# A two-layer encoder on one core: a settled pair's first copy of u goes behind the second product's cast and sum, and two products of the down projections change places

## The chip, the cores and the metric

The kernel runs on one core of a Trainium2 chip. Five engines take part: TensorE (PE; its weight loads are shown as PEld), VectorE (DVE), ScalarE (ACT), GpSimd (POOL) and SyncE (SP, which here only issues DMAs). The metric is the device time of one execution in microseconds (us), as the median of several runs.

## What is computed

The reference is a trunk of two layers over two groups of tokens, 512 and 256, with 1024 features, all in float32. Four of its six phases are feed-forward networks (FFN) of one form:

```python
def swiglu(h, wg, wu, wd):
    return (jax.nn.silu(h @ wg) * (h @ wu)) @ wd

x = x + 0.5 * swiglu(rmsnorm(x, f1_n), f1_g, f1_u, f1_d)
x = x + mixer(rmsnorm(x, mix_n), ...)
x = x + 0.5 * swiglu(rmsnorm(x, f2_n), f2_g, f2_u, f2_d)
```

The inner width is 2816. The mixer of layer 0 joins a gated unit and windowed attention, that of layer 1 is a neighbourhood attention; the change doesn't touch them. A last `rmsnorm` ends the trunk.

## The kernel before

**Precision.** A float32 product is made of three passes. An operand is split into a high part (`whi` for weights, a cast on ScalarE, line 122) and a low part, the operand less its high part (`wlo`, a subtraction on VectorE, line 123). The passes are high by high, high by low, low by high (`mm3`). So a weight block must be cast before the first pass, and its low part made before the third matmul. `whi` and `wlo` have five buffers each. Operands of the activations are split in the same manner by `split` (lines 208 and 209).

**Fewer products.** A pair of 128-wide blocks of the inner width, times two halves of 384 tokens, forms a 2x2 block product. It is done with seven products instead of eight (Winograd's form of Strassen's method). The seven are named after their activation operand: b11, b21, t1, t2, t3, n4, b22. The weight operand of some is a sum, made on VectorE by `sums` (line 739): s1 = a21 + a22, s2 = s1 - a11, s3 = a11 - a21, s4 = a12 - s2 (in the buffer of s2). Products t2, t3, t1, b22 take s2, s3, s1, s4; n4 takes a22. The profile leaves numbers out of names, so that s1, s2 and s4 are all "s"; s3's buffer is "s" too.

**An FFN** has 11 pairs of columns (`pair(p)`), each for `gate` and `up`. The first four pairs are early: their b11 and b21 products run first, and the rest is done in `settle`, in the order t2, t3, n4, t1, b22, gate before up in each. While gate's product runs, `parts` makes the weight operand of the next one. After a t2 or t3 product, `keep` copies the bank into an SBUF tile u (line 573, ScalarE) and takes one step of `operands(p - 1)`. Those steps make the activation operands that the previous pair gives to the down projection: each is a `put` (a cast and a subtraction, lines 208 and 209) or a `sub` (line 497). In the profile these operands are db (b11, b21, b22), dt (t1, t2, t3) and dn (n4). The s1 sums of an early pair come ready from DMAs issued by GpSimd, which add as they write, so that its s2 is one subtraction.

**Down projections.** After pairs 2, 4, 6, 8 the `down` of two finished pairs runs (pairs 0 and 1 behind pair 2, and so on); behind pair 9 stands a `down` of pair 8 alone. It loads two rows of weights for each pair (`raw`, four buffers, issued by SP): row 0 holds a11 and a21, row 1 holds a12 and a22. It makes the seven products for four output blocks each: t1 on banks Z, b11 and b21 on banks X, t2 and t3 on banks Y, b22 on banks W, n4 on banks Y. Y begins as a copy of X, W as a copy of Y after t2. The results are added to the tiles x (line 795, VectorE). X and W lie in PSUM pool `mm`, Y and Z in `aux`; each pool has four banks. The next stage begins with products in `mm`. In the first FFN, SP also issues small loads for bias tables between the others (lines 1634 and 1639).

**Order.** Only TensorE's instructions keep the order in which the code traces them (`manual_schedule` for PE). Those of the other engines are put in order when the program is built, by the framework's scheduler, which goes by readiness and by the order of tracing. `issue_after(ins)` makes the instructions traced in its block follow `ins` where they are on the engine of `ins`; it sets an order in the queue and no wait between engines.

Of the kernel before, what the change touches and what calls it, by code (L numbers as in the profile page):

```python
# [14 lines left out]
ALU = mybir.AluOpType  # L15
# [40 lines left out]
class Trunk:  # L56
# [55 lines left out]
    def wsplit(self, src, eng=None, keep=False):  # L112

        nc = self.nc
        self.pi += 1
        if keep:
            hi, lo = (self.fw.tile([P, 512], F32R, tag="s", name=f"k{n}{self.pi}", bufs=8) for n in ("hi", "lo"))
        else:
            hi = self.wp.tile([P, 512], F32R, tag="whi", name=f"whi{self.pi}")
            lo = self.wp.tile([P, 512], F32R, tag="wlo", name=f"wlo{self.pi}")  # L120
        hi, lo = (t.rearrange("p (a b) -> p a b", a=src.shape[1]) for t in (hi, lo))
        nc.scalar.copy(hi, src)  # L122
        (eng or nc.gpsimd).tensor_tensor(out=lo, in0=src, in1=hi.bitcast(F32), op=ALU.subtract)  # L123
        return hi, lo

# [243 lines left out]
    def etile(self, name):  # L369
        return self.fw.tile([P, H], F32, tag="e", name=name, bufs=NE)  # L370
# [107 lines left out]
    def ffn(self, pre):  # L478
        nc = self.nc
# [36 lines left out]
        def operands_2(h, sub, put):  # L516
            h11, h12, h21, h22 = h[0, 0], h[0, 1], h[1, 0], h[1, 1]
            yield put("t2", h11)
            yield sub(h12, h22, h12)
            yield put("t3", h12)  # L520
            yield put("b22", h22)
            yield sub(h21, h21, h11)
            yield put("n4", h21)

        entries, entered, addeds = {}, {}, {}

        def pair(p):
# [13 lines left out]
            s, bank, e = {}, {}, {}  # L541
# [5 lines left out]
            def parts(n, b):  # L547
                name = {"t2": "s2", "t3": "s3", "t1": "s1", "b22": "s4"}.get(b)
                with self.tc.high_priority() if b == "t2" and p in urgent else nullcontext():
                    return self.wsplit(sums(n, name) if name else a[n, 2, 2], nc.vector)  # L550
# [19 lines left out]
            def keep(out, key, n):  # L570

                e[n, out] = etile(out)
                nc.scalar.copy(e[n, out], bank[key, n])  # L573
                next(steps, None)

            def add(key, n, other):
                t = e[n, other]
                nc.vector.tensor_tensor(out=t, in0=bank[key, n], in1=t, op=ALU.add)  # L578
                next(steps, None)

            def hidden(i, half, g, u):

                self.run_until(lambda: half in scales)
                h[i, half] = t = g if half else etile("sg")
                v = u if half else etile("v")
                r = rt[:, HALVES[half][0] : HALVES[half][1]]
                nc.vector.tensor_tensor(out=t, in0=g, in1=r, op=ALU.mult)
                nc.scalar.activation(t, t, AF.Silu)
                self.freed = nc.vector.tensor_tensor(out=v, in0=u, in1=r, op=ALU.mult).ins
                nc.vector.scalar_tensor_tensor(out=t, in0=t, scalar=0.5, in1=v, op0=ALU.mult, op1=ALU.mult)  # L590

            def begin(n, p1):

                bank["Y", n] = self.psum()[:, :H]
                nc.scalar.copy(bank["Y", n], p1)
# [56 lines left out]
            def settle(st):  # L652

                todo = [(n, b) for b in ("t2", "t3", "n4", "t1", "b22") for n in names]
                key = {"t1": "Z", "b22": "Z"}
                for i, (n, b) in enumerate(todo):
                    now, st = st, None
                    if i + 1 < len(todo):
                        st = parts(*todo[i + 1])
                    elif p + 1 < EARLY and (p % 2 or not p):  # L660
                        entered[p + 1] = entries[p + 1]()
                    if b == "t2":
                        begin(n, e[n, "p1"])
                    product(n, None, b, key.get(b, "Y"), b == "t1", now)
                    if b in ("t2", "t3"):
                        keep(b.replace("t", "u"), "Y", n)
                    elif b == "n4":
                        next(steps, None)
                    else:
                        add("Z", n, "u3" if b == "t1" else "u2")  # L670
                    if n == "up":
                        if b == "n4":
                            hidden(1, 0, bank["Y", "gate"], bank["Y", "up"])
                        elif b == "t1":
                            hidden(1, 1, e["gate", "u3"], e["up", "u3"])
                        elif b == "b22":
                            hidden(0, 1, e["gate", "u2"], e["up", "u2"])
# [59 lines left out]
    def sums(self, a11, a12, a21, a22, s, n, name):  # L737

        f = lambda o, x, y, op: self.nc.vector.tensor_tensor(out=o, in0=x, in1=y, op=op)  # L739
        if name == "s1":  # L740
            return s[n, "s1"]
        if name == "s2" and (n, "s1") in s:
            t = s[n, "s2"] = self.fw.tile([P, 4, P], F32, tag="s", name="s2", bufs=8)
            f(t, s[n, "s1"], a11, ALU.subtract)
            return t
        if name == "s4":
            t = s[n, "s2"]
            f(t, a12, t, ALU.subtract)
            return t
        if name == "s2":  # L750
            t = s[n, "s1"] = self.fw.tile([P, 4, P], F32, tag="s", name="s1", bufs=8)
            f(t, a21, a22, ALU.add)
        t = s[n, name] = self.fw.tile([P, 4, P], F32, tag="s", name=name, bufs=8)
        if name == "s3":
            f(t, a11, a21, ALU.subtract)
        else:
            f(t, s[n, "s1"], a11, ALU.subtract)
        return t
# [4 lines left out]
    def down(self, pre, pairs, d, acc, then=None):  # L763

        nc = self.nc
        a, s, bank = {}, {}, {}
        for p in pairs:
            rows = [self.raw(f"{pre}_w_down", 2 * p + k, 1, 0, D)[:, 0, :] for k in (0, 1)]  # L770
            a[p] = [t[:, i * 512 : (i + 1) * 512].rearrange("p (a b) -> p a b", a=4) for i in (0, 1) for t in rows]
        sums = lambda name: {p: self.sums(*a[p], s, p, name) for p in pairs}

        def product(w, b, key, start, out, to=None):

            st = {p: self.wsplit(w[p], nc.vector) for p in pairs}
            for j in range(4):
                new = lambda k: (self.psum(self.aux, "aux") if k in "YZ" else self.psum())[:, :H]
                if start:
                    bank[key, j] = new(key)  # L780
                ps = bank[key, j]
                for p in pairs:
                    self.mm3(
                        ps, (st[p][0][:, j, :], st[p][1][:, j, :]), d[p][b],
                        start and p == pairs[0], p == pairs[-1], not start,
                    )
                if to:
                    bank[to, j] = new(to)
                    nc.scalar.copy(bank[to, j], ps)
                if out:  # L790
                    o = acc[j] if out is acc else self.x[4 * out[0] + j][:, HALVES[out[1]][0] : HALVES[out[1]][1]]
                    if out is acc and pairs[0] == 0:
                        nc.scalar.copy(o, ps)
                    else:
                        nc.vector.tensor_tensor(out=o, in0=ps, in1=o, op=ALU.add)  # L795

        def more(n):
            for _ in range(n if len(pairs) > 1 else 0):
                next(self.later, None)

        w = {n: {p: a[p][i] for p in pairs} for i, n in enumerate(("a11", "a12", "a21", "a22"))}
        s2 = sums("s2")
        if then:
            then()
        product(sums("s1"), "t1", "Z", True, acc)
        product(w["a11"], "b11", "X", True, None, "Y")
        more(3)
        product(w["a12"], "b21", "X", False, (0, 0))
        more(1)
        product(s2, "t2", "Y", False, None, "W")  # L810
        more(3)
        product(sums("s3"), "t3", "Y", False, (1, 1))
        product(sums("s4"), "b22", "W", False, (0, 1))
        product(w["a22"], "n4", "Y", False, (1, 0))

    def last_operands(self, d, k0, h, acc=None):

# [1008 lines left out]
```

## Time and profile before

| | us |
|---|---|
| median of 3 runs | 2592.65 |
| lowest and highest | 2589.17, 2595.09 |
| the profiled execution, its own time | 2590.38 |
| span of the profiled execution | 2588.6 |
| mean granted TensorE clock in it | 0.996 |

A line of the timeline gives the start, the duration, the engine, the line of the kernel, the operation, the tile written and those read, and how many were merged; in brackets stands the idle time of the engine before it, and what ended it. In a window row each engine's busy time stands with the number of its instructions. The first FFN fills the span from its start to about 515 us, the second 780 to 1250, the third 1250 to 1740, the fourth 2100 to the end.

### The profile page before, as it was taken

To read this page: it belongs to the slowest core of one execution; us is meant where nothing else is said; L and a number is where in the kernel's file an instruction comes from. 1 tells how busy PE (TensorE), PEld (TensorE's weight loads), DVE (VectorE), ACT (ScalarE), POOL (GpSimd) and SP (SyncE) were. 2 spreads that over 40 slices of the span, in tenths; PEclk is the share of its full clock that TensorE was granted. 3 is DMA by queue.
4 is the path that set the end of the run, shared out by engine and by line. 5 is a ranking of instruction groups with operands and counts; after the bars stand their busy time and mean duration, and the time that the engine had idled before them with its cause. 6 is when DMAs were issued, how large, how long until landed. Compare 5 with 4: busy or idle time off the path is not lost.

```text
span 2588.6 us, 41317 instructions
## 1 busy us (share of the span) xinstructions
PE 2552.2 (99%) x15114; PEld 2487.2 (96%) x15114; DVE 2232.6 (86%) x4662; ACT 1366.6 (53%) x2869; POOL 155.5 (6%) x252
## 2 busy tenths in 40 slices
PE   8999999999999999999999999999999999999998
PEld 8999999988899999999999999998998999999997
DVE  7988898978879989889998889886776699888897
ACT  7544454646656545445654445454455575444543
POOL 1000000000021000000100000001222220000000
PEclk9999999999999999999999999999999999999999
DMA  7523222331144322222542222242221343222222
GB/s 246 170 81 106 72 74 74 124 100 46 58 125 132 114 66 74 74 66 98 136 109 82 66 77 71 66 145 64 64 64 41 106 134 119 82 74 74 71 66 76
DMA packets 93372, 238.68 MB, mean 92 GB/s; under 512 B 21488, under 2 KB 34288, under 8 KB 93168
## 3 DMA queue, kind: packets, MB, share of 16 engines
q1 hardware_dynamic: 85712, 218.96, 26.3%
q0 software_dynamic: 7168, 16.78, 3.1%
q8 instruction: 119, 1.95, 0.3%
q14 instruction: 85, 0.70, 0.1%
q10 hardware_dynamic: 288, 0.29, 0.0%
HBM read 226.56 MB, written 15.07 MB: 93 GB/s over the span
## 4 chain that ended last, share of the span: by engine, by line
PE 89%; DVE 6%; ACT 2%; DMA 1%; issue 1%; SPq 0%; DVEq 0%; ACTq 0%
PE ps_mm L152 54%; PE ps_aux L152 34%; PE ps_aux L156 1%; DVE wlo L123 1%; ACT p L1109 1%; DVE p L1103 1%; DMA raw<-in_w 1%; DVE tl L209 0%; DMA x<-in_x 0%; DVE tmp L415 0%; DVE p L1119 0%; ACT whi L122 0%; DVE s L739 0%; DMA first<-in_w 0%; DVE o L1254 0%
## 5 line engine op out<-in xcount | busy, mean ns | idle before, releaser
L122 ACT CAST whi<-s 128x512 fp32r<-128x512 f32 x496 | 304.6, 620 | 407.3 <-DVE s L739 177.6
L122 ACT CAST whi<-raw 128x512 fp32r<-128x512 f32 x504 | 306.1, 619 | 222.9 <-PE ps_mm L152 91.3
L123 DVE TENSOR_TENSOR wlo<-s,whi 128x512 fp32r<-128x512 f32 x496 | 336.8, 684 | 61.0 <-ACT whi L122 53.4
L123 DVE TENSOR_TENSOR wlo<-raw,whi 128x512 fp32r<-128x512 f32 x471 | 321.7, 691 | 18.2 <-ACT whi L122 14.5
L152 PE MATMUL ps_mm<-db,whi 128*128 128x384 f32 x864 | 219.2, 334 | 0.0
L152 PE MATMUL ps_aux<-dt,whi 128*128 128x384 f32 x864 | 219.2, 334 | 0.0
L152 PEld LDWEIGHTS ps_aux<-dt,whi 128*128 128x128 f32 x864 | 156.0, 188 | 0.0
L152 PEld LDWEIGHTS ps_mm<-db,whi 128*128 128x128 f32 x864 | 156.0, 188 | 0.0
L152 PE MATMUL ps_mm<-xh,whi 128*128 128x512 f32 (+1 forms) x416 | 146.2, 352 | 0.0
L152 PE MATMUL ps_aux<-dt,wlo 128*128 128x384 f32 x432 | 144.4, 334 | 1.4 <-DVE wlo L123 1.4
L152 PE MATMUL ps_mm<-db,wlo 128*128 128x384 f32 x432 | 144.3, 334 | 0.0
L152 PE MATMUL ps_mm<-xh,wlo 128*128 128x512 f32 (+1 forms) x416 | 141.3, 340 | 0.0
L152 PE MATMUL ps_mm<-xl,whi 128*128 128x512 f32 (+1 forms) x416 | 141.2, 339 | 0.0
L739 DVE TENSOR_TENSOR s<-raw,raw 128x512 f32<-128x512 f32 x124 | 84.0, 685 | 25.7 <-DMA raw<-in_w 25.5
L578 DVE TENSOR_TENSOR u<-ps_aux,u 128x384 f32<-128x384 f32 x176 | 96.9, 550 | 4.9 <-PE ps_aux L152 4.8
L152 PE MATMUL ps_aux<-dh,whi 128*128 128x384 f32 x384 | 97.5, 334 | 0.0
L795 DVE TENSOR_TENSOR x<-ps_aux,x 128x384 f32<-128x384 f32 x160 | 85.3, 551 | 14.1 <-PE ps_aux L152 13.8
L1109 ACT ACTIVATE p<-p,st 128x256 f32<-128x256 f32 (+3 forms) x144 | 68.9, 480 | 49.3 <-DVE st L1107 49.2
L573 ACT COPY u<-ps_mm 128x384 f32<-128x384 f32 x176 | 83.5, 475 | 16.5 <-PE ps_mm L152 15.9
L795 DVE TENSOR_TENSOR x<-ps_mm,x 128x384 f32<-128x384 f32 x160 | 86.1, 550 | 7.1 <-PE ps_mm L152 6.8
L107 POOL DMA_DIRECT2D s<-in_w x64 | 47.1, 781 | 702.2 <-PE ps_aux L152 387.6
L152 PEld LDWEIGHTS ps_mm<-xh,whi 128*128 128x128 f32 x416 | 79.8, 192 | 9.3 <-issue 0.9
(516 smaller groups left out, 8134.1 us busy)
## 6 DMA issues: line engine op xcount, KB each, us to landing
raw<-in_w SPq DMA_DIRECT2D x346, 512.0 KB, 3.7
s<-in_w POOLq DMA_DIRECT2D x64, 256.0 KB, 5.0
xdm<-x SPq DMA_DIRECT2D x16, 384.0 KB, 2.4
x<-in_x SPq DMA_DIRECT2D x16, 192.0 KB, 6.3
tok<-in_xt SPq DMA_DIRECT2D x12, 256.0 KB, 6.5
xold<-xdm SPq DMA_DIRECT2D x8, 384.0 KB, 3.1
x<-xdm SPq DMA_DIRECT2D x8, 384.0 KB, 4.7
out_y<-y SPq DMA_DIRECT2D x8, 384.0 KB, 2.4
```

What stands on the lines that cost most here:

```text
L107: (eng or self.nc.sync).dma_start(raw, src, **kw)
L122: nc.scalar.copy(hi, src)
L123: (eng or nc.gpsimd).tensor_tensor(out=lo, in0=src, in1=hi.bitcast(F32), op=ALU.subtract)
L152: self.nc.tensor.matmul(out, lhsT=lhsT, rhs=rhs, start=start, stop=stop, **kw)
L156: self.nc.tensor.transpose(out, src, self.ident)
L573: nc.scalar.copy(e[n, out], bank[key, n])
L578: nc.vector.tensor_tensor(out=t, in0=bank[key, n], in1=t, op=ALU.add)
L739: f = lambda o, x, y, op: self.nc.vector.tensor_tensor(out=o, in0=x, in1=y, op=op)
L795: nc.vector.tensor_tensor(out=o, in0=ps, in1=o, op=ALU.add)
L1103: nc.vector.tensor_tensor_reduce(out=outs[i], in0=ps_list[i], in1=adds[i], scale=1.0, scalar=init[i], op0=ALU.add, op1=ALU.max, accum_out= ...
L1109: ins = nc.scalar.activation(outs[i], outs[i], AF.Exp, bias=nm[:, i : i + 1], accum_out=sm[:, i : i + 1])
```

## The change

There are four edits. In `settle`, `keep` of gate's t2 (the first of the ten products, `not i`) is traced in a block that puts its ScalarE instructions behind the last cast of a weight operand (`self.cast`, up's at that point) and its VectorE instructions behind the last s2 sum (`self.summed`, up's too). In `operands_2`, n4's two steps come ahead of b22's. In `down`, n4's product precedes b22's. There too the sums s3 and s4 are traced sooner, and the steps of the other pair's operands are taken as 3, 2, 2 instead of 3, 1, 3.

```diff
-        nc.scalar.copy(hi, src)
+        self.cast = nc.scalar.copy(hi, src).ins
         (eng or nc.gpsimd).tensor_tensor(out=lo, in0=src, in1=hi.bitcast(F32), op=ALU.subtract)
...
             yield put("t3", h12)
-            yield put("b22", h22)
             yield sub(h21, h21, h11)
             yield put("n4", h21)
+            yield put("b22", h22)
...
                     if b in ("t2", "t3"):
-                        keep(b.replace("t", "u"), "Y", n)
+                        with ExitStack() as stack:
+                            for ins in (self.cast, self.summed) if not i else ():
+                                stack.enter_context(self.tc.issue_after(ins))
+                            keep(b.replace("t", "u"), "Y", n)
...
         if name == "s2" and (n, "s1") in s:
             t = s[n, "s2"] = self.fw.tile([P, 4, P], F32, tag="s", name="s2", bufs=8)
-            f(t, s[n, "s1"], a11, ALU.subtract)
+            self.summed = f(t, s[n, "s1"], a11, ALU.subtract).ins
             return t
...
         product(w["a11"], "b11", "X", True, None, "Y")
         more(3)
+        s3 = sums("s3")
         product(w["a12"], "b21", "X", False, (0, 0))
-        more(1)
+        more(2)
         product(s2, "t2", "Y", False, None, "W")
-        more(3)
-        product(sums("s3"), "t3", "Y", False, (1, 1))
-        product(sums("s4"), "b22", "W", False, (0, 1))
+        more(2)
+        s4 = sums("s4")
+        product(s3, "t3", "Y", False, (1, 1))
         product(w["a22"], "n4", "Y", False, (1, 0))
+        product(s4, "b22", "W", False, (0, 1))
```

## The prediction

> **What bounds the kernel now.** The page's busy rows and its chain by engine come first:
>
> ```profile
> PE 2552.2 (99%) x15114; PEld 2487.2 (96%) x15114; DVE 2232.6 (86%) x4662; ACT 1366.6 (53%) x2869; POOL 155.5 (6%) x252
> ...
> PE 89%; DVE 6%; ACT 2%; DMA 1%; issue 1%; SPq 0%; DVEq 0%; ACTq 0%
> ```
>
> TensorE is busy for 2552.2 of 2588.6 us, and the change takes no matmul away. Only the 36.4 us in which TensorE stands still, and time at a low clock, can be won. So I next cut the span into windows (length, then busy us of PE, PEld, DVE, ACT, POOL, then granted clock, DMA share, GB/s), and asked whom PE waited for:
>
> ```profile
> 150.00:200.00 50.00, 46.87 (x261) 46.52 (x262) 45.76 (x83) 25.98 (x51) 0.00 (x0) 0.97 0.35 100
> ...
> 250.00:300.00 50.00, 48.55 (x281) 48.23 (x280) 44.73 (x84) 24.54 (x50) 0.00 (x0) 1.00 0.29 88
> ...
> 850.00:900.00 50.00, 50.00 (x290) 50.00 (x290) 43.99 (x81) 26.09 (x53) 2.04 (x3) 1.00 0.42 131
> ```
>
> ```profile
> PE ps_mm L152 <- ACT whi L122: 4.6, 3, 3.5
> ...
> PE ps_aux L152 <- DVE wlo L123: 1.4, 1, 1.4
> ```
>
> Windows like 850 to 900 have no hole. Among the places that the diff touches, 150 to 200 misses 3.13 us and has the one dip of the clock (0.97), and 250 to 300 misses 1.45 us. The timeline of PE shows the first hole. It is the settling of pair 3 in the first FFN, right after the first down projection:
>
> ```profile
> 146.58 0.45 PE L152 MATMUL ps_mm<-t20h,whi 128*128 128x384 f32 x1
> ...
> 149.00 0.34 PE L152 MATMUL ps_mm<-t23h,wlo 128*128 128x384 f32 x1
> 152.81 0.45 PE L152 MATMUL ps_mm<-t20h,whi 128*128 128x384 f32 x1 [3.47 <-ACT whi L122]
> 153.09 0.36 PE L152 MATMUL ps_mm<-t20l,whi 128*128 128x384 f32 x1
> 153.78 0.69 PE L152 MATMUL ps_mm<-t20h,wlo 128*128 128x384 f32 x1 [0.33 <-DVE wlo L123]
> ...
> 156.94 0.34 PE L152 MATMUL ps_mm<-t30h,whi 128*128 128x384 f32 x1
> ```
>
> ```profile
> 891.60 0.33 PE L152 MATMUL ps_mm<-t20h,whi 128*128 128x384 f32 x1
> ...
> 895.76 0.33 PE L152 MATMUL ps_mm<-t30h,whi 128*128 128x384 f32 x1
> ```
>
> The second fence is pair 3 of the second FFN: its two t2 products (gate and up, 24 matmuls) take 895.76 - 891.60 = 4.16 us, 0.173 a matmul. In the first FFN they take 156.94 - 146.58 = 10.36. The loss is **6.20 us**, and splits at the same pitch: gate's product 149.17 - 146.58 = 2.59 instead of 2.08 (0.51 lost), then 152.81 - 149.17 = 3.64 of wait, then up's product 4.13 instead of 2.08. Of these last 2.05, the wait for wlo is 153.78 - 153.09 - 0.17 = 0.52; the other 1.53 is clock:
>
> ```profile
> 152.80:156.90 4.10, 3.77 (x12) 3.42 (x13) 3.36 (x6) 1.18 (x2) 0.00 (x0) 0.58 0.57 150
> ```
>
> Who made up's operand late? ScalarE and VectorE in that stretch:
>
> ```profile
> 149.37 0.48 ACT L573 COPY u<-ps_mm 128x384 f32<-128x384 f32 x1 [2.84 <-PE ps_mm L152]
> 149.75 0.51 ACT L208 CAST db<-sg 128x384 fp32r<-128x384 f32 x1
> 152.14 1.22 ACT L122 CAST whi<-s 128x512 fp32r<-128x512 f32 x2 [1.88 <-DVE s L739]
> ```
>
> ```profile
> 147.17 0.55 DVE L795 TENSOR_TENSOR x<-ps_aux,x 128x384 f32<-128x384 f32 x1
> 147.64 0.68 DVE L739 TENSOR_TENSOR s<-raw,s 128x512 f32<-128x512 f32 x1
> 150.29 0.56 DVE L209 TENSOR_TENSOR db<-sg,db 128x384 fp32r<-128x384 f32 x1 [1.97 <-ACT db L208]
> 150.89 0.56 DVE L497 TENSOR_TENSOR sg<-u,sg 128x384 f32<-128x384 f32 x1
> 151.36 0.68 DVE L739 TENSOR_TENSOR s<-s,raw 128x512 f32<-128x512 f32 x1
> 151.97 0.68 DVE L739 TENSOR_TENSOR s<-raw,raw 128x512 f32<-128x512 f32 x1
> ```
>
> It is a ring. Up's s2 (151.36) stands in VectorE's queue behind db's low half (150.29), which waits for ScalarE's cast of db (149.75), which stands behind the copy of gate's u (149.37), which waits for gate's product to end. So up's operand is begun only when its product should be running.
>
> **The change, part by part.** No instruction is added or removed; all costs are of order.
>
> *The hold.* In 16 settlings, `keep` of gate's u2 goes behind up's cast on ScalarE, and the operand step in it (db's cast and low half) behind the last s2 sum on VectorE. That breaks the ring. In pair 3 of the first FFN the sum can start where VectorE comes free: at 147.64, or at 148.24 behind the sum that stands there. The cast then starts at 148.4 to 149.0 (151.36 to 152.14 is 0.78), the low half at 149.1 to 149.7; gate's product ends at 149.17, and up's third matmul, the first that reads wlo, is due at 149.52. Remaining wait here: 0.3 to 1.0. Queued behind the held copy are the db cast and then t3's casts; they are delayed by no more than that cast (0.62, half of the 1.22 for two), since the copy could not start before 149.2 anyway. Next late is t3 of gate, due at 151.3 to 152: if its sum (now at 151.97, directly behind up's s2) keeps that neighbour, its low half is ready near 151 and nothing is lost. If db's low half and the subtraction precede it, it starts at about 151.2, its cast at 152, its low half at 152.7: a wait of up to 1.4. So what remains lies between 0.3 and 2.4; I take 0.8, nearer to the neighbour order and to the second FFN, which loses nothing. In the other 15 settlings the products leave no such gap. There up's cast is already ahead of the copy, or PE would have waited, so I cost the hold at zero, covered by the 2.08 us of gate's product; without that cover it costs the cast, 0.62.
>
> *The order n4, b22 and the sums.* From the first down projection:
>
> ```profile
> 120.07 0.68 DVE L739 TENSOR_TENSOR s<-raw 128x512 f32<-128x512 f32 x1
> ...
> 134.84 0.68 DVE L123 TENSOR_TENSOR wlo<-raw,whi 128x512 fp32r<-128x512 f32 x1
> ...
> 138.42 0.69 DVE L123 TENSOR_TENSOR wlo<-raw,whi 128x512 fp32r<-128x512 f32 x1 [0.50 <-ACT whi L122]
> ```
>
> ```profile
> 135.55 0.33 SPq L107 DMA_DIRECT2D raw<-in_w  x1
> ...
> 139.14 0.33 SPq L107 DMA_DIRECT2D raw<-in_w  x1
> ```
>
> ```profile
> 134.04 0.51 PE L152 MATMUL ps_aux<-dt,whi 128*128 128x384 f32 x2
> ...
> 142.36 0.51 PE L152 MATMUL ps_aux<-dn,whi 128*128 128x384 f32 x2
> ```
>
> s3 is formed at 120.07 though its product starts at 134.04: the scheduler already runs it 14 us early, so tracing it sooner is worth about nothing. n4 is different. Its splits (134.84, 138.42) are the last readers of two raw buffers, and the SP queue issues the next two loads right behind them (135.55, 139.14). n4's product moves ahead by one product (from 142.36 by 4.16), so these loads start up to 4.16 us sooner. Pair 3's third and fourth weight tiles come sooner too, which makes the hold safer; elsewhere they were in time. The operand steps carry the same six pieces in another order, n4's one piece sooner: zero. SP issues the same loads in the same order.
>
> The sum: -(3.64 + 0.52 + 1.53) + 0.8 = **-4.9 us**, with 0.51 left at gate's start. The profiled run took 2590.38 us (span 2588.6), 2.27 below the median 2592.65 but inside its runs; the difference goes over whole: 2592.65 - 4.9 = **2587.8 us**.
>
> [...] The idle of 3.47 was followed by a clock of 0.58; that of 1.45 below was followed by 1.00:
>
> ```profile
> 292.56 0.45 PE L152 MATMUL ps_aux<-dt,wlo 128*128 128x384 f32 x1 [1.45 <-DVE wlo L123]
> ```
>
> ```profile
> 292.60:295.20 2.60, 2.60 (x15) 2.60 (x16) 2.60 (x6) 0.00 (x0) 0.00 (x0) 1.00 0.00 0
> ```
>
> So a remaining wait under 1.45 costs only itself. [...]
>
> **The rivals.**
> 1. *The clock drop is not in every run.* Then unprofiled runs of before have not paid the 1.53, and the gain is 4.9 - 1.5 = 3.4: 2589.3. For it: the idle from which the clock drops lies between 1.45 and 3.47; if it is close to the latter, small shifts from run to run decide. Against: the one look shows the drop.
> 2. *The wait moves to t3.* Db's pieces precede gate's s3: 2.4 remain, the gain is 5.69 - 2.4 = 3.3; with a further 1.0 lost on up's t3, 2.3: 2590.4. For it: VectorE stands idle until 150.29 for db, so a scheduler may well fill in what is ready by then. Against: the two sums are neighbours now.
> 3. *The hole at 292.56 goes too,* since the reordered queues change what VectorE does before the second down projection: 4.9 + 1.45 = 6.35, 2586.3. Against: that wait lies ahead of all that the diff moves there.
> 4. *The hold does nothing,* because up's s2 still comes late for want of a buffer or a load: 2592.7. Against: the ring explains the row, and the loads were issued by 139.14, 12 us earlier.
> 5. *Slower: n4 now follows t3 on the same four banks.* Its first matmul on a bank overwrites the sum that t3's add (1,1) must read first; before, b22 lay between. It is tight in the four down projections of a single pair:
>
> ```profile
> 447.81 0.51 PE L152 MATMUL ps_mm<-db,whi 128*128 128x384 f32 x2
> ...
> 449.89 0.51 PE L152 MATMUL ps_aux<-dn,whi 128*128 128x384 f32 x2
> ...
> 451.97 0.33 PE L152 MATMUL ps_mm<-b110h,whi 128*128 128x384 f32 x1
> ```
>
> ```profile
> 447.06 1.94 DVE L795 TENSOR_TENSOR x<-ps_aux,x 128x384 f32<-128x384 f32 x4
> 448.92 1.94 DVE L795 TENSOR_TENSOR x<-ps_mm,x 128x384 f32<-128x384 f32 x4
> 450.78 1.94 DVE L795 TENSOR_TENSOR x<-ps_aux,x 128x384 f32<-128x384 f32 x4
> ```
>
> n4 will start at 447.81 (where b22 did), and the first add (1,1) ends at 447.06 + 0.55 = 447.61: 0.2 us to spare, 0.2 to 0.4 on the other banks (pitch 0.465 of adds against 0.52 of products). Likewise b22's adds, now last at 450.78, free the first bank for the next stage at 451.3, 0.65 before 451.97. It decides at a delay of 0.2: if one more low half (0.68) and two sums (0.68 each) precede the adds, each place loses 2.04 - 0.2 = 1.8 us, four places 7.4, and without the hold's gain the time is 2592.65 + 7.4 = 2600.0; with it 2595.1. In the two-pair down projections a bank has twice the time, and I see no price.
>
> **How the numbers follow.** The forecast 0.50; rival 1 0.15, rival 2 0.14, rival 3 0.08, rival 4 0.08, rival 5 0.05. The range 2584.5 to 2594.0: down past rival 3 by the scatter of a median (three runs of before lie 5.9 apart), up past rival 4 by 1.3; outside are rival 5, some of 4 and the tails, some 15 in 100. About 0.2%, 5.2 us, is what a measurement of this kernel can tell from no change, so "faster" begins at 2587.5, just below the forecast. Two fifths of the forecast's chance (0.21), nearly all of rival 3 (0.07) and a little of the others (0.05) make 0.33 faster; slower, above 2597.8, is rival 5 without the gain and a tail: 0.05; the rest is 0.62.
>
> **What would show it.** Right: in the first FFN's pair 3, t3 starts 4.5 to 6.6 us after t2 (now 10.36), the copy of u stands behind two casts, the window there has clock 1.00; SP's loads move from 135.55 and 139.14 to about 131.5 and 135. Wrong: PE again waits over 2 us between gate's and up's t2, or new waits stand at n4 behind t3 (about 447.8) or at the stage behind a down projection. New waits in stretches that are now without a hole, from queues that come out otherwise than I assume, would spoil the sum.

## The result and the profile after

| | us |
|---|---|
| after, median of 21 runs (lowest to highest) | 2594.53 (2589.11 to 2598.1) |
| before, median of 21 runs beside it | 2590.77 (2587.76 to 2595.09) |
| ratio after to before, with its 95% interval | 1.0014, 1.0008 to 1.002 |
| span of the profiled execution, after and before | 2592.8 and 2588.6 |

The change costs some 3.6 us; 4.9 us of gain were forecast. The 21 runs of before also put its median 1.9 us below that of the three runs known ahead.

First the page of after (busy us, share and count for each engine; the chain by engine), then PE's row of waits by releaser (us in total, times, longest):

```profile
PE 2556.8 (99%) x15114; PEld 2488.9 (96%) x15114; DVE 2228.3 (86%) x4662; ACT 1365.6 (53%) x2869; POOL 155.3 (6%) x252
...
PE 83%; DVE 10%; DMA 3%; ACT 2%; issue 1%; SPq 0%; DVEq 0%; ACTq 0%
```

```profile
PE ps_aux L152 <- ACT whi L122: 2.8, 1, 2.8
...
PE ps_aux L152 <- DVE u L578: 2.5, 6, 1.2
...
PE ps_aux L156 <- DVE o L1330: 1.7, 1, 1.7
...
PE ps_mm L152 <- ACT whi L122: 1.5, 3, 0.6
```

The wait for `whi` on `ps_mm` that headed the list of before (4.6 us, longest 3.5) has shrunk to 1.5. In its place stand one of 2.8 us on `ps_aux`, six waits for L578's sum into u, and one of 1.7 in the first mixer. The chain has lost 6 points of PE to DVE and DMA. PE's busy time grew by 4.6 us with the same 15114 matmuls; more of them ran at half clock, 61 in after's three stretches at it against 47 in before's four (listed at the end).

**Where it was won.** Pair 3 of the first FFN after the change, from the timelines of PE, ACT, DVE and SP, and the window over the two t2 products:

```profile
144.16 0.45 PE L152 MATMUL ps_mm<-t20h,whi 128*128 128x384 f32 x1
...
147.28 0.44 PE L152 MATMUL ps_mm<-t20h,whi 128*128 128x384 f32 x1 [0.37 <-ACT whi L122]
...
149.86 0.33 PE L152 MATMUL ps_mm<-t30h,whi 128*128 128x384 f32 x1
```

```profile
146.61 0.62 ACT L122 CAST whi<-s 128x512 fp32r<-128x512 f32 x1 [2.50 <-DVE s L742]
147.14 0.47 ACT L573 COPY u<-ps_mm 128x384 f32<-128x384 f32 x1
147.51 0.51 ACT L208 CAST db<-sg 128x384 fp32r<-128x384 f32 x1
```

```profile
145.82 0.68 DVE L742 TENSOR_TENSOR s<-s,raw 128x512 f32<-128x512 f32 x1
...
148.60 0.55 DVE L209 TENSOR_TENSOR db<-sg,db 128x384 fp32r<-128x384 f32 x1
```

```profile
130.02 0.33 SPq L107 DMA_DIRECT2D raw<-in_w  x1
...
132.53 0.33 SPq L107 DMA_DIRECT2D raw<-in_w  x1
```

```profile
144.10:149.80 5.70, 5.12 (x25) 4.09 (x25) 5.46 (x10) 1.95 (x5) 0.00 (x0) 1.00 0.30 77
```

Up's s2 (145.82) now precedes db's low half (148.60), up's cast (146.61) precedes the copy of u (147.14), and the clock is 1.00. From t2 to t3 it takes 149.86 - 144.16 = 5.70 us instead of 10.36.

**Where it was lost.** The table takes the same matmul in both timelines. The offset is its start after less its start before; each step is the change of the offset since the row above.

| matmul | before | after | offset | step |
|---|---|---|---|---|
| pair 3, gate's t2 | 146.58 | 144.16 | -2.42 | -2.42 |
| pair 3, gate's t3 | 156.94 | 149.86 | -7.08 | -4.66 |
| start of the next stage | 231.84 | 224.91 | -6.93 | +0.15 |
| third down projection, behind t1 | 295.97 | 293.46 | -2.51 | +4.42 |
| behind the first mixer | 780.56 | 780.18 | -0.38 | +2.13 |
| second FFN, pair 3, gate's t2 | 891.60 | 891.70 | +0.10 | +0.48 |
| the same, behind b22 | 937.67 | 938.49 | +0.82 | +0.72 |
| fourth FFN, start | 2102.75 | 2104.77 | +2.02 | +1.20 |
| the same, b22 of an earlier pair | 2180.30 | 2183.29 | +2.99 | +0.97 |
| the same, behind the next b22 | 2234.54 | 2238.68 | +4.14 | +1.15 |

The first step is the loads at the start, which differ between executions: before, run again (e8 below), stands at -2.63 at the same matmul. Nor can the step of 1.20 ahead of the fourth FFN be put down to the change: e8 has 0.80 there. The largest loss is at the place of the 1.45 us hole. That is the third down projection, of pairs 4 and 5 (the prediction and the first expectations call it the second). The hole in after, with the windows behind it, then DVE there in after and in before:

```profile
286.59 1.01 PE L152 MATMUL ps_aux<-dt,whi 128*128 128x384 f32 x2 [2.76 <-ACT whi L122]
```

```profile
286.60:290.00 3.40, 3.18 (x9) 2.68 (x10) 3.22 (x6) 1.50 (x3) 0.00 (x0) 0.50 0.22 35
290.00:292.80 2.80, 2.80 (x11) 2.80 (x10) 1.79 (x4) 0.00 (x0) 0.00 (x0) 0.52 0.75 219
```

```profile
283.34 0.56 DVE L589 TENSOR_TENSOR v<-ps_mm,acc 128x384 f32<-128x384 f32 x1 [1.52 <-PE ps_mm L152]
284.01 0.56 DVE L590 SCALAR_TENSOR_TENSOR sg<-sg,v 128x384 f32<-128x384 f32 x1
284.67 0.56 DVE L209 TENSOR_TENSOR dt<-sg,dt 128x384 fp32r<-128x384 f32 x1
285.15 0.68 DVE L742 TENSOR_TENSOR s<-raw,raw 128x512 f32<-128x512 f32 x1
```

```profile
288.68 0.68 DVE L739 TENSOR_TENSOR s<-raw,raw 128x512 f32<-128x512 f32 x1
290.28 0.56 DVE L589 TENSOR_TENSOR v<-ps_mm,acc 128x384 f32<-128x384 f32 x1 [0.92 <-PE ps_mm L152]
```

This is a second ring of the same kind. `v` waits for the last product of the stage, n4 of up. The next product, t1, begins with pair 4, whose operand is ready; the sum s1 of pair 5 comes next, and it needs nothing of the stage that ends. Its weights were there. SP issued the last of those loads in after at 274.70, and the page's median from issue to landing is 3.7 us, so by this estimate it had landed some 5 us ahead of `v`:

```profile
274.70 0.33 SPq L107 DMA_DIRECT2D raw<-in_w  x1
```

Before, s1 (288.68) stood ahead of `v` (290.28); after, it stands three instructions behind it (285.15 against 283.34), and VectorE waits 1.52 us for PE with s1 undone. So PE waits 2.76 us instead of 1.45, and this time the clock halves behind it: 1.3 us of wait more, and 3.1 of clock and of small waits in its wake, make the 4.42. No line of the diff is about s1, t1 or `v`; the scheduler, run again, ordered it otherwise.

### The profile page after: what moved, and what is told of

The parts are those of the page before. It is cut to its first block, busy times and chain, and to the rows that moved or that the text cites. A ratio compares the mean times of both kernels' runs of the same rounds, so it can differ in the third digit from the quotient of the medians.

```text
span 2592.8 us, 41348 instructions
## 1 busy us (share of the span) xinstructions
PE 2556.8 (99%) x15114; PEld 2488.9 (96%) x15114; DVE 2228.3 (86%) x4662; ACT 1365.6 (53%) x2869; POOL 155.3 (6%) x252
## 4 chain that ended last, share of the span: by engine, by line
PE 83%; DVE 10%; DMA 3%; ACT 2%; issue 1%; SPq 0%; DVEq 0%; ACTq 0%
PE ps_mm L152 50%; PE ps_aux L152 32%; DVE wlo L123 2%; DMA raw<-in_w 2%; PE ps_aux L156 1%; ACT p L1114 1%; DVE s L742 1%; DVE p L1108 1%; DVE tmp L415 1%; DVE tl L209 0%; DMA x<-in_x 0%; ACT whi L122 0%; DVE p L1124 0%; DVE o L1259 0%; DVE acc L235 0%
## 5 line engine op out<-in xcount | busy, mean ns | idle before, releaser
L578 DVE TENSOR_TENSOR u<-ps_aux,u 128x384 f32<-128x384 f32 x176 | 96.8, 550 | 4.5 <-PE ps_aux L152 4.4
L742 DVE TENSOR_TENSOR s<-s,raw 128x512 f32<-128x512 f32 x124 | 84.7, 683 | 4.0 <-DMA raw<-in_w 3.5
```

## The experiments

Each kernel was timed against the kernel before on the same chip (ratios with 95% intervals). Theory A is the three local terms: the ring in pair 3, the ring at the third down projection, waits at b22.

**e1: the hold alone.** Its edits are the three below, against before.

```diff
-        nc.scalar.copy(hi, src)
+        self.cast = nc.scalar.copy(hi, src).ins
...
-                        keep(b.replace("t", "u"), "Y", n)
+                        with ExitStack() as stack:
+                            for ins in (self.cast, self.summed) if not i else ():
+                                stack.enter_context(self.tc.issue_after(ins))
+                            keep(b.replace("t", "u"), "Y", n)
...
-            f(t, s[n, "s1"], a11, ALU.subtract)
+            self.summed = f(t, s[n, "s1"], a11, ALU.subtract).ins
```

> The hold alone; the order of the products, of the operand pieces and of the sums is that of before. Theory A (order of queues, three local terms): the ring in the first FFN's pair 3 is broken, t3 starts 5.5 to 6 us after t2 instead of 10.36 (-4.7), but the scheduler, re-run, puts the s1 sum of the second down projection behind the wait for v on VectorE, so that the hole there (1.45 us, clock 1.00) becomes about 2.8 us with a clock near 0.5 behind it (+4.4); no waits at b22 in the down projections. Net of these -0.3: ratio to before 0.9995 to 1.0005. Theory B (the loss belongs to the swapped products alone, and the hold is a clean gain): second down projection as before, net -4.7, ratio 0.998.

Ratio 1.0007, 0.9998 to 1.0015. The hole is that of after (PE's timeline):

```profile
288.36 0.62 PE L152 MATMUL ps_aux<-dt,whi 128*128 128x384 f32 x2 [2.76 <-ACT whi L122]
```

By the offsets this execution won 4.6 us in pair 3 and lost 3.8 here. Theory B, a clean gain of 4.7, falls. In the trace the hold moves instructions of VectorE, ScalarE and SP (some bias loads) in the first FFN alone, up to and in this down projection; behind it every engine has the order of before. So the hold reaches some 140 us behind the place where it works, and that was far enough.

**e2: the swap alone.**

```diff
-        product(sums("s4"), "b22", "W", False, (0, 1))
         product(w["a22"], "n4", "Y", False, (1, 0))
+        product(sums("s4"), "b22", "W", False, (0, 1))
```

> Only n4's product goes ahead of b22's in the down projections. Theory A: t2 to t3 in the first FFN's pair 3 stays near 10.4 us; the hole at the start of the second down projection grows to about 2.8 us with the clock drop (+4.4), and b22 in the settlings behind the down projections of the second and fourth FFN waits 0.2 to 1.2 us for VectorE's sum into u (+1.2 and +2.1, as in after): about +7.7, ratio 1.003. Theory B (n4 behind t3 must wait for the sums of t3 on the same banks): as much or more, but as waits of n4's first matmuls on the sums into x, and none at the second down projection's start.

Ratio 1.0059, 1.0046 to 1.0072: twice what theory A said. The hole of 2.76 us is there too, and n4 nowhere waits. What no theory had stands behind each of the four down projections of a single pair (first place, PE and DVE):

```profile
457.07 0.44 PE L152 MATMUL ps_mm<-b110h,wlo 128*128 128x384 f32 x1 [0.90 <-DVE wlo L123]
```

```profile
450.22 4.11 DVE L795 TENSOR_TENSOR x<-ps_aux,x 128x384 f32<-128x384 f32 x8
454.30 2.12 DVE L795 TENSOR_TENSOR x<-ps_mm,x 128x384 f32<-128x384 f32 x4
456.33 1.28 DVE L123 TENSOR_TENSOR wlo<-raw,whi 128x512 fp32r<-128x512 f32 x2
```

The sums of b22 into x, now the last of twelve, stand in front of the split for the next stage's b110. That costs 1.18 us by the offsets, four times (e10's text, on record before that run, takes 1.06). More of this execution's time went in the mixers; see e7 and e8.

**e3: the order of the pieces, and s3 and s4 sooner, alone.**

```diff
-            yield put("b22", h22)
             yield sub(h21, h21, h11)
             yield put("n4", h21)
+            yield put("b22", h22)
...
+        s3 = sums("s3")
...
-        more(1)
+        more(2)
...
-        more(3)
-        product(sums("s3"), "t3", "Y", False, (1, 1))
-        product(sums("s4"), "b22", "W", False, (0, 1))
+        more(2)
+        s4 = sums("s4")
+        product(s3, "t3", "Y", False, (1, 1))
+        product(s4, "b22", "W", False, (0, 1))
```

> Only the order of the operand pieces, s3 and s4 traced sooner, and the counts of pieces between products; no hold, and b22's product ahead of n4's as before. Theory A and theory B: both say that these move nothing: hole of 3.5 us between the t2 products, hole of 1.45 at the second down projection, no wait at b22; ratio 0.9995 to 1.0005. If it is slower by 0.1% instead, the sums made sooner crowd VectorE and both theories miss a term.

Ratio 1.0001, 0.9992 to 1.0009, with holes of 3.47 and 1.45 us as in before. By themselves these edits do nothing, as both theories said.

**e4: the change again.**

> The changed kernel once more. Both theories: ratio 1.0014 as before. The second look is to tell which terms of the ledger repeat: theory A has the ring's gain (-4.7), the second down projection's loss (+4.4) and the waits at b22 (+1.2, +2.1) in every look, and takes the -2.5 us at the start and the about +4.5 us in the first mixer for differences between executions, which need not come again; theory C takes these two for parts of the change: then they come again at the same size.

Ratio 1.0016, 1.0008 to 1.0025. The gain in pair 3, the hole of 2.76 and the waits at b22 came again; so did the -2.5 us at the start and the loss in the first mixer, which counted against taking these for scatter. e8 settles the start, and e7 and e8 look at the mixer.

**e5 and e12: the hold, and the sums of the third down projection first.** To e1 is added (`wsplit` keeps its low half's instruction as `self.low`, and `product` takes the ready split `self.st1` for t1):

```diff
+    def begin_down(self, pre, pairs):
+        a, s = {}, {}
...
+        s2 = {p: self.sums(*a[p], s, p, "s2") for p in pairs}
+        self.st1 = {p: self.wsplit(s[p, "s1"], self.nc.vector) for p in pairs}
+        return a, s, s2
...
-                hidden(1, 0, bank["Y", "gate"], bank["Y", "up"])
+                if p < NPAIR - 1 and p == 6 and self.ffns == 1:
+                    self.rows2[p - 2, p - 1] = self.begin_down(pre, range(p - 2, p))
+                begun = self.rows2.get((p - 2, p - 1))
+                with self.tc.issue_after(self.low) if begun else nullcontext():
+                    hidden(1, 0, bank["Y", "gate"], bank["Y", "up"])
...
-        a, s, bank = {}, {}, {}
+        bank = {}
+        a, s, s2 = self.rows2.pop(tuple(pairs), None) or self.begin_down(pre, pairs)
```

> The hold alone as in e1_hold_only, and in the first FFN's third down projection (the one that the prediction called the second) the sums and the split of the first product are traced ahead of the last gated product of the stage before, and that product's wait for v is issued behind them. Theory A (what the hold lost is the order of that sum behind the wait for v): t2 to t3 in pair 3 stays near 5.9 us, the hole at about 286 us (2.76 us and the half clock behind it) is gone, and so is the 1.45 us that before had there: net -4.4 - 1.5 = about -6 against before, ratio 0.9975 to 0.9985. Rival (the hole there has another cause, say the loads of those rows): the hole stays at 1.4 to 2.8 us, ratio 1.000 to 1.001 as in e1.

> The fastest kernel so far once more. Theory A: -6, ratio 0.9967 to 0.9985 again.

Ratios 0.9976 (0.9967 to 0.9985) and 0.9983 (0.9974 to 0.9992): faster than both kernels, by 4.4 to 6.2 us against before. DVE at that place in e5, and the window over it:

```profile
281.46 0.68 DVE L748 TENSOR_TENSOR s<-raw,raw 128x512 f32<-128x512 f32 x1
...
283.39 0.68 DVE L124 TENSOR_TENSOR wlo<-s,whi 128x512 fp32r<-128x512 f32 x1
...
284.46 0.55 DVE L591 TENSOR_TENSOR v<-ps_mm,acc 128x384 f32<-128x384 f32 x1
```

```profile
280.00:290.00 10.00, 10.00 (x60) 10.00 (x59) 9.83 (x19) 5.73 (x12) 0.00 (x0) 1.00 0.18 52
```

Sum and split are done when `v` comes, and PE has no hole. The loads were not the cause: they are issued in the same order. That settles the term: order alone, undone by order alone.

**e6: the change with the same repair.**

> The whole change with the same repair at the third down projection. Theory A: -6 as in e5, and the waits at b22 in the second and fourth FFN (+1.2, +2.1) stay, since they come from the swapped products: about -2.7, ratio 0.999. Rival as in e5: ratio 1.0014 as the change has it.

Ratio 0.9988, 0.9979 to 0.9997, as theory A had it. Above e5 and e12 lies what the swap still costs, 0.0005 to 0.0012, that is 1.3 to 3.1 us, though the intervals overlap. By the offsets it is some 1.4 us, around b22 of pair 3 in two FFNs: in the second e6's offset to before changes by 0.05 and e5's by -0.31, in the fourth e6's by 1.05 and e5's by -0.02. Here the fourth, in e6 and in after:

```profile
2226.01 0.45 PE L153 MATMUL ps_aux<-b220h,whi 128*128 128x384 f32 x1 [0.34 <-DVE u L580]
```

```profile
2233.92 0.44 PE L152 MATMUL ps_aux<-b220h,whi 128*128 128x384 f32 x1 [0.40 <-DVE u L578]
...
2236.49 0.41 PE L152 MATMUL ps_aux<-b220h,whi 128*128 128x384 f32 x1 [0.21 <-DVE u L578]
```

In `settle`, b22 writes the bank Z that t1 left, and must wait for VectorE's sum from it into u (L578). In all six profiled kernels with the swap PE waits here in the fourth FFN, 0.34 to 1.72 us at the first; in all eight executions without it there is no wait at this place. The timelines show what stands behind the late sum into u (VectorE in after, then in before):

```profile
2225.49 0.69 DVE L742 TENSOR_TENSOR s<-raw 128x512 f32<-128x512 f32 x1 [1.76 <-DMA raw<-in_w]
```

```profile
2220.70 0.69 DVE L123 TENSOR_TENSOR wlo<-s,whi 128x512 fp32r<-128x512 f32 x1 [0.92 <-ACT whi L122]
```

With the swap, sums stand further ahead in VectorE's queue, and one of them waits for its load: 1.54 to 2.63 us in all six. In the eight without it VectorE waits 0.92 us for a cast instead, and for no load in the 20 us ahead of this b22. The three longest waits for the load (2.35 to 2.63) go with the three longest of PE (1.41 to 1.72), but that the load alone makes them was not tried apart. PE's wait at 2183 is another matter: there VectorE waits for a load in every execution, before too, and PE for 0.2 to 1.2 us.

**e7 and e11: the repair alone. e8: before again.**

> The repair alone, without any part of the change. Theory A: the ring in pair 3 stays (10.36 us from t2 to t3), the hole of 1.45 us at the third down projection goes: -1.5, ratio 0.9994. Rival: no difference, the hole stays.

> The repair alone once more. Theory D (the half clock in the first mixer falls early, at about 580 us, or late, behind a wait of 1.66 us, by where the grid of 3.413 us lies in that execution): the median may come out 1.5 us below before or up to 2 above, and this look may show either. Rival (the kernel's own time of arrival at the mixer, 1.5 us sooner, makes it late): late again, median 2592 to 2593, ratio 1.0005 to 1.0012.

> The kernel before once more, for a second look. Theory D: the loss of about 2.5 us in the first mixer that after shows in both looks, and e1 and e2 too, is no matter of order (the instructions there stand in the same order on every engine): it hangs on where a grid of 3.413 us falls on which TensorE's granted clock is set, and that starts anew in each execution. Then this look may show the half clock at about 582 us or at about 596 us, behind a wait of 1.66 us. If it is at 582 to 587 again, as in the first look and in e3, the phase of the grid is not left to chance, and the term belongs to the change in a way that I do not see yet.

Ratios 1.0006 (0.9997 to 1.0015) and 1.0000 (0.9992 to 1.0009) for the repair, 1.0003 (0.9993 to 1.0014) for before. The hole of 1.45 is gone in e7 and e11 (some 1.0 us net by the offsets, 0.7 being given back at 294), yet nothing is won. The first mixer shows why; e7, then e8, timeline of PE and windows:

```profile
580.49 0.44 PE L153 MATMUL ps_aux<-kh,q 64*128 64x384 f32 x1 [0.23 <-DVE st L1115]
594.12 0.66 PE L157 MATMUL ps_aux<-ident,p 128*128 128x128 f32 x4 [1.66 <-DVE o L1337]
```

```profile
580.00:584.00 4.00, 3.77 (x28) 3.26 (x29) 3.44 (x12) 3.98 (x7) 0.00 (x0) 1.00 0.00 0
...
596.00:600.00 4.00, 4.00 (x20) 4.00 (x20) 3.89 (x9) 0.00 (x0) 0.00 (x0) 0.50 0.20 28
```

```profile
580.48 0.59 PE L152 MATMUL ps_aux<-kh,q 64*128 64x384 f32 x1 [0.24 <-DVE st L1103]
594.53 0.66 PE L156 MATMUL ps_aux<-ident,p 128*128 128x128 f32 x4 [0.65 <-DVE o L1325]
```

```profile
580.00:584.00 4.00, 3.76 (x17) 3.08 (x17) 3.44 (x12) 3.42 (x6) 0.00 (x0) 0.58 0.00 0
...
596.00:600.00 4.00, 4.00 (x39) 3.59 (x37) 4.00 (x10) 0.00 (x0) 0.00 (x0) 1.00 0.17 15
```

The two reach this place within 0.01 us of each other, with the same instructions in the same order. In e8 the clock halves at once, PE falls back, and its next wait for VectorE is 0.65. In e7 it keeps its clock, comes sooner, waits 1.66, and the clock halves behind that, for longer. Call e8's the early form and e7's the late one. Inside the mixer, at e8's 759 us, e7 is 3.6 us later, and at the mixer's end, at 779, still 2.8. So this step is the clock, not the order. What goes with either form is set out at the end; the loss of 2.13 there in after is of this kind. Whether a kernel's own time of arrival makes the late form likelier stays open. Both executions of the repair had it, and so had both of the change (after, e4) and both of the hold with the repair (e5, e12); both of before had not. So no kernel was seen in both forms. The repair's two ratios lie 1 to 2.5 us above what the local terms give, each within its interval of them or nearly so.

**e9: everything but the hold. e10: the same with s3 and s4 where they were.** e9 is the diff of the change without its hunk in `settle`; e10 is against e9:

```diff
-        s3 = sums("s3")
...
-        s4 = sums("s4")
-        product(s3, "t3", "Y", False, (1, 1))
+        product(sums("s3"), "t3", "Y", False, (1, 1))
         product(w["a22"], "n4", "Y", False, (1, 0))
-        product(s4, "b22", "W", False, (0, 1))
+        product(sums("s4"), "b22", "W", False, (0, 1))
```

> The whole change without the hold. Theory A: the ring in pair 3 stays (10.4 us from t2 to t3, half clock behind it); the sum at the third down projection is behind the wait for v all the same, because the swap alone already moves it there (+4.4); waits at b22 behind the down projections of the second and fourth FFN (+1.6 to +3.3, as in e6 and after); the four waits of 0.90 us at b110 behind the single-pair down projections of e2 are not there, since s4 is made ahead: +6 to +7.7, ratio 1.0023 to 1.003. Rival (the hold is needed for the loss at the third down projection): ratio 1.0006 to 1.0013, hole of 1.45 us there.

> As e9, but s3 and s4 are traced where before traced them. Theory A: s4 stands so late on VectorE that the split for the next stage's b110 comes behind the twelve sums into x: the four waits of 0.90 us (1.06 with what follows) at b110 behind the single-pair down projections are there as in e2, +4.2 on top of e9: ratio 1.004 to 1.0055. Rival (the order of the operand pieces mends them): no such waits, ratio as e9.

e9: ratio 1.0025, 1.0016 to 1.0034. e10: 1.006, 1.0042 to 1.0079. PE in e9 at the third down projection; in e9's window behind the first single-pair down projection; and in e10 at that place:

```profile
291.50 0.62 PE L152 MATMUL ps_aux<-dt,whi 128*128 128x384 f32 x2 [2.76 <-ACT whi L122]
```

```profile
446.00:456.00 10.00, 10.00 (x59) 9.99 (x58) 9.75 (x20) 3.05 (x7) 0.00 (x0) 1.00 0.16 52
```

```profile
455.15 0.44 PE L152 MATMUL ps_mm<-b110h,wlo 128*128 128x384 f32 x1 [0.90 <-DVE wlo L123]
```

The second ring closes without the hold too. With the hold the whole change has 1.0014 to 1.0016, so in this company the hold is worth 2.3 to 2.8 us by the ratios and 4.7 by the timelines; the intervals, some 2.3 us to either side, hold both. The four waits at b110 are in e10 and not in e9: s4 made sooner leaves VectorE room for the next stage's split ahead of the sums into x. So these four waits (4.7 us) come with the swap and go with s3 and s4. e10, which rests on two runs, lies further above e9 than that, some 9 us: its first mixer had the late form, that of e9 the early one.

## Why the prediction was wrong

**The hold** was right in mechanism, place and size. From t2 to t3 it is 5.70 us (4.5 to 6.6 forecast). The wait left is 0.37 where 0.8 was taken, the clock is 1.00, and the gain is 4.66 of 4.9. Rival 4 falls with it, and so does rival 2: from t3 to the start of the next stage the offset changes by 0.15 alone. SP's two loads moved from 135.55 and 139.14 to 130.02 and 132.53, by 3.1 and 4.2 more than the start had moved.

**The step that failed** is the one under rival 3, "Against: that wait lies ahead of all that the diff moves there", together with "all costs are of order" being booked only where the diff stands. The place was named, and its price was on the page (1.45 us). But it was seen as a possible gain alone. Everything that the scheduler orders behind an edit can be moved by it. The prediction's last sentence named such a loss, but the sum and the chances gave it nothing. The hold alone (e1) and the swap alone (e2) each turned s1 behind `v`, and the change paid 4.42 for it; e5 shows the sign that rival 3 had in mind. With that term, -4.9 + 4.4, the forecast would have come out at about no change.

**The swap, costed at zero,** was the second mis-sized term: 1.3 to 3.1 us by e6 against e5 and e12. "In the two-pair down projections a bank has twice the time, and I see no price" looked at the banks of the down projection itself. The price lies in the settlement behind it, where b22 waits for L578. The table's steps for the hold, the second ring and these two places, -4.66 + 4.42 + 0.72 + 1.15, make 1.6 us; measured are 3.6, with an interval from 2.1 to 5.2. What makes up the rest is not shown; the loss in the first mixer, 2.13 here and 2.4 in e4, may be part of it.

**The sums,** "worth about nothing", are worth nothing only without the swap (e3). With it they save the four waits at b110 (e10 against e9). So of two edits costed at zero, one costs 4.7 us that the other takes away.

**Rival 5** fell as written. All of n4's products in after, from the groups of PE (busy us, mean ns, idle us before them):

```profile
L152 PE MATMUL ps_aux<-dn,whi 128*128 128x384 f32 x288 | 73.1, 334 | 0.0
```

No n4 waits for the sums of t3. Its second half, b22's sums "now last", did bite in e2 and e10, through VectorE's queue and not through the bank.

**Rival 1** fell: all eight profiled executions with the ring have the half clock behind it, for 3.41 us from 153.28 in before, 150.53 in e8 and 152.31 in e11.

**What was left to chance** is as large as the effect. The base was a median of three runs, 1.9 us above that of 21. The first mixer moves by 2.8 us between kernels with the same order in it (e7 and e8), and how much of that is chance stays open.

## What to carry to other kernels

Where a scheduler orders the queues, an edit is not costed until the new queues have been compared with the old ones everywhere: look for each sum, split or cast that needs nothing of the running product and has come to stand behind an instruction that waits for it. Such a ring is best broken by hand at each place where it can close, as e5 does, since the next edit may close it again. Two edits that are free one by one can be dear or cheap as a pair, so test the pair.

## What the runs showed of the hardware

The traces record the granted clock in stretches. Those at half clock (start in us from the start of the span, and length) in before, after, e8 and e11, without the one that begins at the end of the work:

```
before  26.98 +3.41   153.28 +3.41   583.36 +3.41   634.56 +3.41
after  285.88 +6.83   596.49 +6.83   634.04 +3.41
e8     150.53 +3.41   580.62 +3.41   631.82 +3.41
e11     26.02 +3.41   152.31 +3.41   596.04 +10.24  637.00 +3.41
```

In each of these four executions the starts differ by whole multiples of 3.413 us (before: 37, 126 and 15 of them), and the lengths are one, two or three times that; where the starts lie differs from execution to execution. What sets them is not shown.

From 20 us on, three of PE's waits in the FFNs of before and after had a half clock at their end or within 0.5 us behind it: 3.35 us (before, until 26.86), 3.47 (before, until 152.81) and 2.76 (after, until 286.59). The longest of the others, 1.45 (before, until 292.56), had none. The step from 1.45 to 2.76 cost 4.42 us in after and 3.8 in e1 by the offsets, not 1.3. In the first mixer 1.44 us (before, until 632.63) and 1.42 (after, until 632.88) were followed by a half clock, so the length of one wait alone does not decide. That the mixers' smaller matmuls are the reason is not shown.

In the first mixer three short waits (0.62, 0.23 and 0.23 or 0.24 us) lie within 2.7 us. What follows is an estimate, counted back from the half clocks above in steps of 3.413 us. In the early form all three lie in one step, 579.94 to 583.36 in before and 577.21 to 580.62 in e8, and the half clock begins where that step ends. In the late form they are split: in after a step begins at 579.42, between the second and the third; in e7, where a clock of 0.94 from 594 to 596 us puts the start of the half clock at about 595.76, one begins at about 578.7, between the first and the second. The clock stays at 1.00 there, and the wait of 1.66 us comes later with its own half clock. That this decides the form is not shown.
